# Eighteen steps of a 128-step product loop computed earlier, in plain fp32, kept in DRAM and read back

## The chip, the core and the metric

The kernel runs on one core of a Trainium2 chip. The metric is device time in microseconds (us). A profiled execution gives the trace that is read here. The engines are named as in the trace: PE (TensorE; PEld is its weight load), DVE (VectorE), ACT (ScalarE), POOL (GpSimd) and SP (the queue that issues most of the transfers). All data are 4-byte floats. Two kinds of product occur on PE: a plain fp32 product, and a product of operands that were cast to the format fp32r.

## The reference, cut to what matters

Two transformer blocks run one after the other on 512 tokens of 1024 channels. The change concerns the last layer, a sparse FFN with 16384 experts of one hidden unit each:

```python
q = (xb @ w_query).reshape(128, 8, 2, 128)
sc = einsum('thpd,hpkd->thpk', q, sub_keys)        # 128 keys in each half
s_top, i_top = lax.top_k(sc, 16)
...                                                # 16 best pairs per head, softmax g
u = jnp.take(expert_u, eidx, axis=0)               # 128 experts per token
h = jax.nn.gelu(jnp.einsum('thkd,td->thk', u, xb))
vv = jnp.take(expert_v, eidx, axis=0)
return jnp.einsum('thk,thkd->td', g * h, vv)
```

## The kernel before, in words

Everything ahead of `phase_d` is unchanged. `phase_d` computes the sparse FFN in three stages that overlap.

- **Query stage** (`d_norm`, `d_query`). The normed input is held transposed as a sum of two fp32r tiles, `hTh` (high part) and `hTl` (low part). PE makes the queries, and DVE finds the 16 best keys and pairs (`top16`, the tile `eq`).
- **Gate stage** (`d_gates`, three calls, one for each of the first three blocks of 128 tokens). For those 384 tokens the layer is computed densely: the gates are spread over all 128 x 128 experts. For each token a one-hot matrix `o1` and a weighted one-hot matrix `o2`, each 128 x 128, are made on ACT, POOL and DVE, and PE multiplies them into PSUM (`pw`, L1280; 384 products, of plain fp32). ACT copies the result to `wst` and SP writes it to DRAM (`w_d`, 12 transfers of 2 MB). Both `o1` and `o2` have three buffers, each for four tokens.
- **Main loop** over 128 steps s, each with 128 experts. SP loads 128 rows of `peer_v` (`vraw`) and, every fourth step, gates (`wb`). The activations `G` of the step are multiplied by the gates (`A`, DVE), both `vraw` and `A` are split into a high and a low fp32r part (`vh`, `vl`, `ah`, `al`), and PE adds 18 products of 512 columns into six PSUM banks (`pY`, L1146).

The activations of a step come from `h_step`: SP loads 128 columns of `peer_u` transposed (`uraw`, three buffers), ACT casts the high part `uh`, POOL subtracts to make the low part `ul` (L1061), PE makes 24 products of 384 columns (`ph`, L1088: hi x hi, hi x lo and lo x hi for eight blocks of channels), and ACT applies Gelu into `G` (L1091). `h_step` runs LA = 33 steps ahead of the step that uses it: the first 33 are written in the gate stage, the others one for each step of the main loop, as long as s + LA is below 128. `G` has LA + 1 buffers.

The last 128 tokens are done by gathering instead: POOL gathers 128 + 128 times one expert row for each token (`X`, `xg`; six buffers), and DVE makes one dot product (L1123) or one weighted sum (L1128) from each, called a dot below. These 256 dots are spread over the main loop by `done`: a step with an `h_step` has weight 2 in `cost`, a step without one has weight 1, and `q` advances by 260 times the share of the weights done so far. DVE's order within the main loop is as written (`manual_schedule`): `vl`, `A`, `al`, then the dots of the step. The other orders are set by a scheduler when the program is built, which may move instructions of later steps ahead where buffers allow.

Of the kernel before, what the change touches and what calls it, by code (L numbers as in the profile page):

```python
# [5 lines left out]
F32 = mybir.dt.float32  # L6
# [3 lines left out]
AF = mybir.ActivationFunctionType  # L10
# [147 lines left out]
class K:  # L158
# [904 lines left out]

    def phase_d(self):
        tc, nc, I, V, C, X = self.tc, self.nc, self.I, self.V, self.C, self.X
        ND, LA, NB, GL = 384, 33, 4, 5
        x_d = self.x_d
        self.w_d = self.dr.tile([32, 128, ND, 4], F32, name="w_d")
        with tc.tile_pool(name="d1", bufs=1) as d1, tc.tile_pool(name="hps", bufs=2, space=PSUM) as hps:
            hh = d1.tile([128, 8, 512], F32R, name="hTh")  # L1070
            hl = d1.tile([128, 8, 512], F32R, name="hTl")
# [8 lines left out]
            def h_step(s):  # L1080
                u = d1.tile([128, 8, 128], F32, name="uraw", bufs=3)
                nc.sync.dma_start(u.rearrange("p k e -> p (k e)"), I["put"][s])
                uh, ul = self.split(d1, "u", u, [128, 8, 128], eng=nc.gpsimd)
                p = hps.tile([128, ND], F32, name="ph")
                n = 0
                for k in range(8):
                    for l, r in ((uh, hh), (uh, hl), (ul, hh)):
                        nc.tensor.matmul(p, l[:, k, :], r[:, k, 0:ND], start=(n == 0), stop=(n == 23))  # L1088
                        n += 1
                G = d1.tile([128, ND], F32, name="G", bufs=LA + 1)  # L1090
                nc.scalar.activation(G, p, AF.Gelu_apprx_tanh)  # L1091
                return G

            with tc.tile_pool(name="dk", bufs=1) as dk, tc.tile_pool(name="kps", bufs=3, space=PSUM) as ps:
                self.ei = dk.tile([128, 4, 128], F32, name="ei")
                self.gt = dk.tile([128, 4, 128], F32, name="gt")
                self.arp = ps
                with tc.tile_pool(name="dn", bufs=1) as dn:
                    self.d_norm(dn, hh, hl, x3, h3)
                with tc.tile_pool(name="dq", bufs=1, reuse_waits="tile") as dq:  # L1100
                    self.d_query(dq, ps, hh, hl)
                with tc.tile_pool(name="dt", bufs=1, reuse_waits="tile") as dt:
                    for t in range(3):
                        self.d_gates(dt, ps, t)
                    Gs = {s: h_step(s) for s in range(LA)}

            def gather(tab, q):
                i = q % 6
                u = X[:, i, :] if i < 4 else xg[:, i - 4, :]
                nc.gpsimd.indirect_dma_start(out=u, out_offset=None, in_=tab,  # L1110
                                             in_offset=bass.IndirectOffsetOnAxis(ap=self.eix[q // 128][:, q % 128:q % 128 + 1], axis=0))
                return u

            with tc.tile_pool(name="dg", bufs=1) as dg, tc.tile_pool(name="yps", bufs=1, space=PSUM) as yps:
                xg = dg.tile([128, 2, 1024], F32, name="xg")
                ug = {}
                cost = [2 if s + LA < 128 else 1 for s in range(128)]
                done = lambda s: min(256, 260 * sum(cost[:s]) // sum(cost))

                def dot(q):  # L1120
                    u = ug.pop(q)
                    if q < 128:
                        nc.vector.scalar_tensor_tensor(u, u, 1.0, h3, op0=OP.mult, op1=OP.mult, accum_out=hv[:, q:q + 1])  # L1123
                        if q == 127:
                            nc.scalar.activation(hv, hv, AF.Gelu_apprx_tanh)
                            nc.vector.tensor_mul(hv, hv, self.g3)
                    else:
                        nc.vector.scalar_tensor_tensor(x3, u, hv[:, q - 128:q - 127], x3, op0=OP.mult, op1=OP.add)  # L1128

                pY = [[yps.tile([128, 512], F32, name=f"pY{t}{h}") for h in range(2)] for t in range(3)]  # L1130
                with tc.manual_schedule(engines={mybir.EngineType.DVE}):
                    for s in range(128):
                        vr = dg.tile([128, 1024], F32, name="vraw", bufs=3)
                        nc.sync.dma_start(vr, I["pv"][s * 128:s * 128 + 128, :])
                        if s % NB == 0:
                            wb = dg.tile([128, ND, NB], F32, name="wb", bufs=2)
                            nc.sync.dma_start(wb, self.w_d[s // NB])
                        vh, vl = self.split(dg, "v", vr, [128, 1024], bufs=3)
                        A = dg.tile([128, ND], F32, name="A", bufs=2)
                        nc.vector.tensor_mul(A, Gs.pop(s), wb[:, :, s % NB])  # L1140
                        ah, al = self.split(dg, "a", A, [128, ND], bufs=3)
                        for t in range(3):
                            for h in range(2):
                                n = 0
                                for l, r in ((ah, vh), (ah, vl), (al, vh)):
                                    nc.tensor.matmul(pY[t][h], l[:, t * 128:t * 128 + 128], r[:, h * 512:h * 512 + 512],  # L1146
                                                     start=(s == 0 and n == 0), stop=(s == 127 and n == 2))
                                    n += 1
                        if s + LA < 128:
                            Gs[s + LA] = h_step(s + LA)  # L1150
                        for q in range(done(s), done(s + 1)):
                            ug[q] = gather(I["pu"] if q < 128 else I["pv"], q)
                            if q >= GL:
                                dot(q - GL)
                for q in range(256 - GL, 256):
                    dot(q)
                nc.sync.dma_start(self.out[384:512, :], x3)
                for t in range(3):
                    xr = dg.tile([128, 1024], F32, name="vraw", bufs=3)
                    nc.sync.dma_start(xr, x_d[t * 128:t * 128 + 128, :])  # L1160
                    for h in range(2):
                        nc.vector.tensor_add(xr[:, h * 512:h * 512 + 512], xr[:, h * 512:h * 512 + 512], pY[t][h])
                    nc.sync.dma_start(self.out[t * 128:t * 128 + 128, :], xr)
# [147 lines left out]
```

## Time and profile before

| what | value |
|---|---|
| median of three runs | 3338.21 us (3332.45 to 3347.19) |
| the profiled execution: its own time | 3341.98 us |
| its span in the trace | 3340.2 us |
| mean granted TensorE clock | 0.971 of full speed |
| PE busy | 3072.6 us, 92% |
| DVE busy | 1834.3 us, 55% |
| POOL busy | 1144.9 us, 34% |
| ACT busy | 970.9 us, 29% |

Shares are of the whole span. Before about 1960 us the program does the other layers, which the change leaves alone. The query stage runs from about 2000 us, the products of the gate stage from 2272.7 to 2400.7 us, and the main loop from 2417.6 us to the end. In the trace each plain fp32 product shows as two MATMUL instructions, so the 384 products of the gate stage are counted there as 768; an fp32r product shows as one.

### The profile page before, as it was taken

The page shows a single profiled execution, that of the slowest core. Times are in us where ns is not written, and L with a number is a line of the kernel's source. Part 1 is how long each engine was busy: PE and PEld are TensorE (multiplying, and loading weights), DVE is VectorE, ACT ScalarE, POOL GpSimd, SP SyncE. Part 2 cuts the span into 40 slices and gives each one's busy share as a digit, 9 for nine tenths or more (in the row PEclk, how much of TensorE's full clock was granted, in tenths as well). Part 3 has the DMA queues.
Part 4 walks back from the last instruction along what each step waited for, and adds up shares of the span by engine and source line. Part 5 has one row for each costly group of instructions (what it writes and reads, how often), then busy time and mean ns, then how long its engine had stood idle before and what let it go on. Part 6 is the DMA issues. An engine that isn't in the chain of part 4 may idle for free.

```text
span 3340.2 us, 42188 instructions
## 1 busy us (share of the span) xinstructions
PE 3072.6 (92%) x16081; PEld 2166.9 (65%) x16081; DVE 1834.3 (55%) x3590; ACT 970.9 (29%) x1745; POOL 1144.9 (34%) x963
## 2 busy tenths in 40 slices
PE   7999999997888988988979989988799999999998
PEld 6777776572323323323337678887699999999986
DVE  2456656461000000000032658999799988989978
ACT  3333323130000000000022742237733333333332
POOL 0433321010000000000002122679778877777733
PEclk9999999988999999999989999999899999999999
DMA  4221112388999999999952152226788888888877
GB/s 144 104 74 58 61 68 72 109 310 349 427 427 427 427 426 427 428 426 427 427 198 76 44 180 87 76 101 190 226 303 311 310 305 299 303 295 303 285 264 260
DMA packets 193351, 837.85 MB, mean 251 GB/s; under 512 B 16509, under 2 KB 66301, under 8 KB 168446
## 3 DMA queue, kind: packets, MB, share of 16 engines
q1 hardware_dynamic: 153230, 693.52, 53.7%
q0 software_dynamic: 38592, 140.53, 11.9%
q8 instruction: 127, 2.08, 0.2%
q10 hardware_dynamic: 1328, 1.11, 0.1%
q14 instruction: 74, 0.61, 0.0%
HBM read 794.47 MB, written 40.63 MB: 250 GB/s over the span
## 4 chain that ended last, share of the span: by engine, by line
PE 71%; DMA 13%; DVE 11%; ACT 3%; issue 1%; POOL 1%; SPq 0%; DVEq 0%; ACTq 0%; POOLq 0%
PE pY L1146 14%; PE ph L1088 13%; PE pj L306 11%; DMA wt<-in_wu_dram 8%; PE pu L872 5%; PE pd L885 5%; PE pg L872 5%; DMA wt<-in_wg_dram 3%; PE pout L769 2%; PE po L897 2%; PE pj L468 1%; PE pq L626 1%; PE pw L1280 1%; DVE eq L1226 1%; DVE o L1278 1%
## 5 line engine op out<-in xcount | busy, mean ns | idle before, releaser
L876 DVE TENSOR_TENSOR sg<-sg,pu 128x512 f32<-128x512 f32 x32 | 22.0, 688 | 683.9 <-PE pu L872 683.9
L1061 POOL TENSOR_TENSOR ul<-uraw,uh 128x1024 fp32r<-128x1024 f32 x128 | 340.8, 2663 | 130.5 <-ACT uh L1058 128.9
L1088 PE MATMUL ph<-hTh,ul 128*128 128x384 f32 x1024 | 348.5, 340 | 18.3 <-POOL ul L1061 18.2
L1088 PE MATMUL ph<-hTh,uh 128*128 128x384 f32 x1024 | 347.4, 339 | 1.9 <-ACT G L1091 1.9
L1088 PE MATMUL ph<-hTl,uh 128*128 128x384 f32 x1024 | 346.1, 338 | 0.0
L1146 PE MATMUL pY<-vh,ah 128*128 128x512 f32 x768 | 302.4, 394 | 21.4 <-DMA vraw<-in_pv_dram 16.9
L1146 PE MATMUL pY<-vl,ah 128*128 128x512 f32 x768 | 300.7, 392 | 0.0
L872 PE MATMUL pu<-wt,xeT 128*64 128x512 f32 x1024 | 265.0, 622 | 37.4 <-DMA wt<-in_wu_dram 37.3
L1146 PE MATMUL pY<-vh,al 128*128 128x512 f32 x768 | 278.2, 389 | 0.0
L872 PE MATMUL pg<-wt,xeT 128*64 128x512 f32 x1024 | 254.5, 604 | 16.7 <-DMA wt<-in_wg_dram 16.7
L885 PE MATMUL pd<-wt,aT 128*64 128x512 f32 x1024 | 243.9, 597 | 22.6 <-ACT aT L881 22.6
L853 POOL DMA_INDIRECT xe<-h_d,idi x8 | 7.7, 957 | 613.8 <-PE pt L859 580.5
L306 PE MATMUL pj<-hh,wh 128*128 128x512 f32 x528 | 215.3, 408 | 1.8 <-DVE hl L205 1.1
L306 PE MATMUL pj<-hh,wl 128*128 128x512 f32 x528 | 216.3, 410 | 0.0
L872 PEld LDWEIGHTS pu<-wt,xeT 128*64 128x64 f32 x1024 | 86.9, 143 | 199.4 <-issue 148.7
L306 PE MATMUL pj<-hl,wh 128*128 128x512 f32 x528 | 214.5, 406 | 0.0
L1088 PEld LDWEIGHTS ph<-hTh,ul 128*128 128x128 f32 x1024 | 194.1, 190 | 22.9 <-POOL ul L1061 22.7
L1058 ACT CAST vh<-vraw 128x1024 fp32r<-128x1024 f32 x128 | 134.5, 1051 | 252.2 <-PE pY L1146 222.8
L872 PEld LDWEIGHTS pg<-wt,xeT 128*64 128x64 f32 x1024 | 88.0, 139 | 172.4 <-issue 139.5
L1088 PEld LDWEIGHTS ph<-hTh,uh 128*128 128x128 f32 x1024 | 194.3, 190 | 6.3 <-ACT G L1091 2.5
L1088 PEld LDWEIGHTS ph<-hTl,uh 128*128 128x128 f32 x1024 | 194.0, 189 | 3.8
L885 PEld LDWEIGHTS pd<-wt,aT 128*64 128x64 f32 x1024 | 88.8, 136 | 151.0 <-issue 121.0
(435 smaller groups left out, 6172.5 us busy)
## 6 DMA issues: line engine op xcount, KB each, us to landing
wt<-in_wg_dram SPq DMA_DIRECT2D x64, 2048.0 KB
wt<-in_wu_dram SPq DMA_DIRECT2D x64, 2048.0 KB
wt<-in_wd_dram SPq DMA_DIRECT2D x64, 2048.0 KB
uraw<-in_put_dram SPq DMA_DIRECT2D x128, 512.0 KB
vraw<-in_pv_dram SPq DMA_DIRECT2D x128, 512.0 KB
wraw<-in_w_in_dram SPq DMA_DIRECT2D x32, 1024.0 KB
w_d<-wst SPq DMA_DIRECT2D x12, 2048.0 KB
wb<-w_d SPq DMA_DIRECT2D x32, 768.0 KB
```

The costliest lines, as they stand in the source:

```text
L306: nc.tensor.matmul(p, l[:, k, :], r[:, k, :], start=(i == 0), stop=(i == 23))
L468: nc.tensor.matmul(pb, wb[:, k, f * 128:f * 128 + 128], y[:, k, :], start=(k == 0), stop=(k == nk - 1))
L626: nc.tensor.matmul(p[o:o + 64, h, :], lhs(h, o), rhs(h, o), start=True, stop=True)
L769: nc.tensor.matmul(pp[t][h], l[:, ts], r[:, hs], start=(k == 0 and i == 0), stop=(k == 7 and i == 2))
L872: nc.tensor.matmul(dst[e * 64:e * 64 + 64], xT[:, k, e * 64:e * 64 + 64], ww[e][:, k, :], start=(k == 0), stop=(k == 7))
L885: nc.tensor.matmul(pd[h][e * 64:e * 64 + 64], aT[:, k, e * 64:e * 64 + 64], wd[e][:, k, h * 512:h * 512 + 512], start=(c == 0 and k == 0), ...
L897: nc.tensor.matmul(po, oh[:, t * 128:t * 128 + 128], yes[h], start=True, stop=True)
L1058: nc.scalar.copy(hi, src)
L1061: (eng or nc.vector).tensor_sub(lo, src, hi)
L1088: nc.tensor.matmul(p, l[:, k, :], r[:, k, 0:ND], start=(n == 0), stop=(n == 23))
L1146: nc.tensor.matmul(pY[t][h], l[:, t * 128:t * 128 + 128], r[:, h * 512:h * 512 + 512], start=(s == 0 and n == 0), stop=(s == 127 and n == 2))
L1226: nc.vector.tensor_mul(eq, eq, ci[:, t:t + 1, :].to_broadcast([128, 16, NCAND]))
```

## The change

Eighteen steps, s = 35, 39, ..., 103 (`parked`), get their activations in another way. Behind the first LA `h_step`s, within the gate stage, `hTh` and `hTl` are added into one fp32 tile `hTf` (four adds on DVE, four on POOL). For each parked step `uraw` is loaded, PE makes eight plain fp32 products of 384 columns straight from `uraw` and `hTf`, ACT applies Gelu into `Gp` (two buffers), and SP writes it to DRAM (`g_d`). In the main loop, where a parked step's `h_step` stood, SP loads `G` from `g_d`. LA falls from 33 to 32, the parked steps get weight 1 in `cost`, and `G` has 33 buffers.

```diff
-        ND, LA, NB, GL = 384, 33, 4, 5
+        ND, LA, NB, GL = 384, 32, 4, 5
+        parked = range(LA + 3, LA + 3 + 4 * 18, 4)
+        g_d = self.dr.tile([128, 128, ND], F32, name="g_d")
...
                     Gs = {s: h_step(s) for s in range(LA)}
+                    hf = dt.tile([128, 8, ND], F32, name="hTf")
+                    for k in range(8):
+                        (nc.gpsimd if k % 2 else nc.vector).tensor_add(hf[:, k, :], hh[:, k, 0:ND], hl[:, k, 0:ND])
+                    for s in parked:
+                        u = d1.tile([128, 8, 128], F32, name="uraw", bufs=3)
+                        nc.sync.dma_start(u.rearrange("p k e -> p (k e)"), I["put"][s])
+                        p = hps.tile([128, ND], F32, name="ph")
+                        for k in range(8):
+                            nc.tensor.matmul(p, u[:, k, :], hf[:, k, :], start=(k == 0), stop=(k == 7))
+                        G = dt.tile([128, ND], F32, name="Gp", bufs=2)
+                        nc.scalar.activation(G, p, AF.Gelu_apprx_tanh)
+                        nc.sync.dma_start(g_d[s], G)
...
-                cost = [2 if s + LA < 128 else 1 for s in range(128)]
+                cost = [2 if s + LA < 128 and s + LA not in parked else 1 for s in range(128)]
...
-                        if s + LA < 128:
+                        if s + LA in parked:
+                            Gs[s + LA] = d1.tile([128, ND], F32, name="G", bufs=LA + 1)
+                            nc.sync.dma_start(Gs[s + LA], g_d[s + LA])
+                        elif s + LA < 128:
                             Gs[s + LA] = h_step(s + LA)
```

The lines below the change have higher numbers in the new kernel: L1088 becomes L1090, L1280 becomes L1297, L1146 becomes L1160.

The first place is PE's order where the gate products begin. Before, the last `h_step` products stand there and then gate products alone:

```order
4315 L1088 MATMUL ph<-hTh,uh 128x384
4316 L1088 MATMUL ph<-hTl,uh 128x384
4317 L1088 MATMUL ph<-hTh,ul 128x384
4318 L1280 MATMUL pw<-o_13143,o_13142 128x128 x4
4319 L1280 MATMUL pw<-o_13160,o_13159 128x128 x4
4320 L1280 MATMUL pw<-o_13177,o_13176 128x128 x4
4321 L1280 MATMUL pw<-o_13194,o_13193 128x128 x4
```

With the change the plain products (L1116, from `hTf` and `uraw`) alternate with them, ten between each twelve gate products further on:

```order
4210 L1090 MATMUL ph<-hTh,ul 128x384
4211 L1116 MATMUL ph<-hTf,uraw 128x384 x2
4212 L1273 MATMUL ptr<-con,f_i 128x128 x2
4213 L1273 MATMUL ptr<-con,gt 128x128
4214 L1116 MATMUL ph<-hTf,uraw 128x384 x12
4215 L1297 MATMUL pw<-o_13093,o_13092 128x128 x4
4216 L1297 MATMUL pw<-o_13110,o_13109 128x128 x4
4217 L1297 MATMUL pw<-o_13127,o_13126 128x128 x4
4218 L1116 MATMUL ph<-hTf,uraw 128x384 x2
4219 L1297 MATMUL pw<-o_13144,o_13143 128x128 x4
4220 L1297 MATMUL pw<-o_13161,o_13160 128x128 x4
4221 L1116 MATMUL ph<-hTf,uraw 128x384 x8
```

All 144 plain products stand among the first 200 of the 384 gate products, as do 72 products of the last three early `h_step`s; the other 184 gate products stand alone behind them. Ahead of the gate products stand 50 `h_step` products fewer than before (456 before, 406 now, in the last long row of them).

The second place is POOL's order in the main loop, where it alternates between gathers (`X`, `xg`) and `ul`. Before there is one `ul` for each step, with two or three gathers between:

```order
429 L1061 TENSOR_TENSOR ul<-uraw,uh 128x1024
430 L1110 DMA X<-in_pu_dram,eix_11227 128x1024 x2
431 L1061 TENSOR_TENSOR ul<-uraw,uh 128x1024
432 L1110 DMA X<-in_pu_dram,eix_11227 128x1024 x2
433 L1061 TENSOR_TENSOR ul<-uraw,uh 128x1024
434 L1110 DMA xg<-in_pu_dram,eix_11227 128x1024 x2
435 L1110 DMA X<-in_pu_dram,eix_11227 128x1024
436 L1061 TENSOR_TENSOR ul<-uraw,uh 128x1024
```

With the change one `ul` in four is gone in the first 72 steps, and up to five gathers stand in a row in its place:

```order
434 L1061 TENSOR_TENSOR ul<-uraw,uh 128x1024
435 L1124 DMA X<-in_pu_dram,eix_11228 128x1024 x4
436 L1124 DMA xg<-in_pu_dram,eix_11228 128x1024
437 L1061 TENSOR_TENSOR ul<-uraw,uh 128x1024
438 L1124 DMA xg<-in_pu_dram,eix_11228 128x1024
439 L1061 TENSOR_TENSOR ul<-uraw,uh 128x1024
440 L1124 DMA X<-in_pu_dram,eix_11228 128x1024 x2
441 L1061 TENSOR_TENSOR ul<-uraw,uh 128x1024
```

The third place is SP's queue in the main loop, here with the change: in a parked step a small load of `G` stands where a load of `uraw` stood.

```order
258 L1151 DMA wb<-w_d 128x1536
259 L1084 DMA uraw<-in_put_dram 128x1024
260 L1148 DMA vraw<-in_pv_dram 128x1024
261 L1084 DMA uraw<-in_put_dram 128x1024
262 L1148 DMA vraw<-in_pv_dram 128x1024
263 L1165 DMA G<-g_d 128x384
264 L1084 DMA uraw<-in_put_dram 128x1024
```

Before, loads of `uraw` and `vraw` alternate there without a break.

## Rows read from the trace of the kernel before

**Rows 1.** Busy time of each engine by stretch: gate stage, gap, main loop, tail.

```profile
core 0: us, PE busy (x) PEld busy (x) DVE busy (x) ACT busy (x) POOL busy (x), PEclk, DMA share, GB/s
2264.00:2401.00 137.00, 115.03 (x824) 104.31 (x822) 132.89 (x463) 119.84 (x319) 129.85 (x197) 0.96 0.68 198
2401.00:2418.00 17.00, 0.41 (x1) 0.41 (x2) 2.40 (x3) 2.31 (x4) 1.97 (x2) 0.58 0.84 273
2418.00:3190.00 772.00, 772.00 (x3917) 704.72 (x3917) 689.57 (x639) 276.87 (x377) 578.58 (x308) 1.00 0.85 301
3190.00:3335.00 145.00, 139.11 (x597) 111.78 (x595) 122.24 (x134) 46.91 (x61) 53.59 (x32) 0.99 0.74 265
```

**Rows 2.** Chain that ended last, main loop: start, us, engine, line, count.

```profile
2443.99 4.17 PE ph L1088 x24
2448.16 4.08 PE pY L1146 x18
```

**Rows 3.** PE's products of L1088 by stretch, before and in the main loop.

```profile
1960.00:2418.00 458.00, 163.17 (x864) 153.93 (x864) 0.96 0.44 141
2418.00:3335.00 917.00, 398.49 (x2208) 385.84 (x2208) 1.00 0.83 295
```

**Rows 4.** Timeline of PE: start, us, line, operation, count, idle time before.

```profile
2178.30 0.44 PE L1088 MATMUL ph<-hTh,uh 128*128 128x384 f32 x1 [1.18 <-ACT G L1091]
...
2263.91 0.38 PE L1256 MATMUL ptr<-con,f_i 128*128 128x128 f32 x2
...
2304.42 4.01 PE L1280 MATMUL pw<-o,o 128*128 128x128 f32 x32 [0.79 <-ACT o L1275]
...
2396.41 4.33 PE L1280 MATMUL pw<-o,o 128*128 128x128 f32 x32 [0.49 <-ACT o L1275]
...
2417.59 0.79 PE L1146 MATMUL pY<-vh,ah 128*128 128x512 f32 x1 [16.85 <-DMA vraw<-in_pv_dram]
```

**Rows 5.** PE's products of L1280 alone, in two stretches of the gate stage.

```profile
2320.00:2360.00 40.00, 34.90 (x256) 31.12 (x256) 1.00 0.73 205
2360.00:2400.00 40.00, 34.46 (x252) 31.14 (x252) 0.96 0.75 210
```

**Rows 6.** Plain fp32 products of another layer (24): durations, first and last start.

```profile
L468 PE MATMUL pj<-zrw,wb x48: 592/592/697, 626.0 to 646.2; 128*128 128x512 f32 x48
```

**Rows 7.** Timeline of POOL at the start of the gate stage.

```profile
2263.85 0.94 POOL L1110 DMA_INDIRECT X<-in_pu_dram,eix  x1 [0.30 <-issue]
2264.82 4.68 POOL L1061 TENSOR_TENSOR ul<-uraw,uh 128x1024 fp32r<-128x1024 f32 x2
```

**Rows 8.** Timeline of DVE in the main loop.

```profile
2603.81 1.21 DVE L1061 TENSOR_TENSOR vl<-vraw,vh 128x1024 fp32r<-128x1024 f32 x1
2604.95 0.84 DVE L1140 TENSOR_TENSOR A<-G,wb 128x384 f32<-128x384 f32 x1
2606.37 0.56 DVE L1061 TENSOR_TENSOR al<-A,ah 128x384 fp32r<-128x384 f32 x1 [0.58 <-ACT ah L1058]
2606.84 1.22 DVE L1123 SCALAR_TENSOR_TENSOR X<-X,h 128x1024 f32<-128x1024 f32 x1
2607.99 0.08 DVE L1123 DVE_READ_ACCUMULATOR X<-X,h 128x1 f32 x1
2607.99 3.43 DVE L1123 SCALAR_TENSOR_TENSOR X<-X,h 128x1024 f32<-128x1024 f32 x1
2611.34 0.08 DVE L1123 DVE_READ_ACCUMULATOR X<-X,h 128x1 f32 x1
2611.34 1.22 DVE L1061 TENSOR_TENSOR vl<-vraw,vh 128x1024 fp32r<-128x1024 f32 x1
```

**Rows 9.** Timeline of POOL in the same stretch of the main loop.

```profile
2607.37 2.96 POOL L1061 TENSOR_TENSOR ul<-uraw,uh 128x1024 fp32r<-128x1024 f32 x1 [0.75 <-ACT uh L1058]
2610.48 1.76 POOL L1110 DMA_INDIRECT X<-in_pu_dram,eix  x1
```

**Rows 10.** Timeline of DVE in the tail, where no `h_step` is left.

```profile
3211.54 1.28 DVE L1128 SCALAR_TENSOR_TENSOR x<-X,hv,x 128x1024 f32<-128x1024 f32 x1
3212.73 1.22 DVE L1061 TENSOR_TENSOR vl<-vraw,vh 128x1024 fp32r<-128x1024 f32 x1
...
3215.82 1.28 DVE L1128 SCALAR_TENSOR_TENSOR x<-X,hv,x 128x1024 f32<-128x1024 f32 x1
3217.01 1.22 DVE L1061 TENSOR_TENSOR vl<-vraw,vh 128x1024 fp32r<-128x1024 f32 x1
```

**Rows 11.** Transfers that SP issued at the end of the gate stage.

```profile
2401.39 0.36 SPq L1283 DMA_DIRECT2D w_d<-wst  x1
2410.25 0.34 SPq L1134 DMA_DIRECT2D vraw<-in_pv_dram  x1
```

## The prediction

> **What bounds the kernel now.** I read the busy time by stretch first [rows 1]. From 2418 to 3190 us PE is busy for all of 772 us: the main loop is bound by PE. DVE is busy there for 689.6 of 772 us, which is 89%. The gate stage, 2264 to 2401 us, is bound by no single engine: DVE is busy for 132.9 and POOL for 129.9 of 137 us, ACT for 119.8, PE for 115.0. Between the two lies a gap of 17 us in which PE does nothing. After 3190 us no `h_step` is left.
>
> The chain of waits gives the prices of the loop: 24 products of an `h_step` take 4.17 us, the 18 products of `pY` 4.08 us [rows 2], so a step is 8.25 us. Of the 128 `h_step`s 36 (864 products) are done before 2418 us and 92 (2208) in the loop [rows 3], since the scheduler moves three more ahead than are written in the gate stage. 92 x 4.17 + 128 x 4.08 = 906 us of PE work fill the 917 us from 2417.6 us to the end.
>
> DVE has to be looked at more closely, because its 89% leave out its waits. One step with two dots [rows 8]: from `vl` at 2603.81 to the next `vl` at 2611.34 is 7.53 us. One dot takes 1.15 us (2606.84 to 2607.99), the other 3.35 us (2607.99 to 2611.34), and while it lasts POOL does its `ul` (2607.37, 2.96 us) [rows 9]. Without dots the step is 7.53 - 1.15 - 3.35 = 3.03 us, DVE's wait of 0.58 us for `ah` included. So a step without dots costs DVE 3.03 us, a dot 1.15 us, and each `ul` of POOL lengthens one dot by 2.20 us. With 260/223 = 1.166 dots for each unit of weight, a step of weight 2 has 2.33 dots: 3.03 + 2.33 x 1.15 + 2.20 = 7.91 us, against PE's 8.25. DVE is only 4% behind PE.
>
> **The price of a plain product.** The kernel before has no plain product of 384 columns. The nearest row is one of 512 columns in another layer [rows 6]: 24 products show as 48 instructions, which start from 626.0 to 646.2 us, so one instruction follows the other after 20.2 / 47 = 0.430 us. Scaled to 384 columns that is 0.322 us, two of them 0.645 us for a product, and 8 x 0.645 = 5.16 us for a parked step. The split step that it replaces takes 4.17 us. The plain step saves the cast and the subtraction on ACT and POOL, but costs PE a quarter more. Over all: 144 x 0.645 = 92.9 us of PE work come, 18 x 4.17 = 75.1 us go.
>
> The Trainium skill states in FP8 and Floating Point Precision, TensorE Precision Notes, that true fp32 takes four passes through the array, and in TensorE: Matmul & The Clock Gate, Back-to-back issue gap, that a pass of N columns takes N/2.4 + 2.5 ns at the full clock. By these an fp32r product of 384 columns would take 162.5 ns, where the row has 4.17 / 24 = 174 ns; a plain one 650 ns; the 17 steps that leave the loop would be worth 66.3 us where the row makes 70.9, and the sum below would come out 5 us later. The measured row is used.
>
> **Gate stage: what is added.** First `hTf`: four adds on DVE and four on POOL. DVE's nearest row is `al` of the same size, 0.56 us [rows 8]. POOL does 1024 columns in 4.68 / 2 = 2.34 us [rows 7], so 384 in 0.9 us, and its adds stand behind four gathers of which the last ends at 2264.8 us. The first plain products can thus run from about 2266 us, where the transposes of the gates began at 2263.9 us [rows 4]. The 50 `h_step` products that no longer stand ahead of them (8.7 us) give nothing: PE waits for `hTf` and for DVE's query work.
>
> From 2266 us PE has, among the first 200 gate products: 92.9 us of plain products, 72 x 0.174 = 12.5 us of split products, and 200 gate products. A gate product is two instructions, and 32 of these take 4.01 to 4.33 us back to back [rows 4], so 0.26 us each, 52 us. Together 157.4 us. Before, gate products went at (256 + 252) / 2 = 254 in 80 us [rows 5], 0.315 us each, a pace that DVE, POOL and ACT set; for 200 that is 63 us. So here PE sets the pace and the others wait. With the three buffers of `o1` and `o2` they are ready for each group of twelve while PE does ten plain products (6.5 us). What PE may wait for is the Gelu that frees `ph` (two buffers): one such wait is 1.18 us [rows 4], so 0 to 21 us for 18 steps; I take 4 us, nearer to nothing, because a buffer is free for most of a step ahead. The 18 loads of `uraw` and 18 writes of `g_d` (13 MB) lie beside 157 us of PE work. The end of this part: 2266 + 157 + 4 = 2427 us. The other 184 gate products go as before, 184 x 0.315 = 58 us: 2485 us, where the last one now ends at 2400.7. **Plus 85 us** (81 to 102).
>
> The gap behind it stays: SP's last write of `w_d` is issued at 2401.39 us, the next load of `vraw` only at 2410.25 [rows 11], and the first `pY` starts at 2417.6 [rows 4]. The same writes and loads end the stage with the change.
>
> **Main loop: what is removed.** Early `h_step`s are 35 now (LA is one less), so 110 - 35 = 75 split steps stay in the loop, 17 fewer: 17 x 4.17 = 70.9 us of PE work. For PE alone that is the gain. But the dots remain 256 in number, and weights of 206 instead of 223 make it 1.262 for each unit. In four steps with one parked (weight 7, 8.83 dots) DVE needs 4 x 3.03 + 8.83 x 1.15 + 3 x 2.20 = 28.9 us, and PE 3 x 8.25 + 4.08 = 28.8. DVE's slack is gone. There are 18 such groups. They take DVE 520 us, PE only 506 us, as three steps were done early: 14 us are given back, and I add 5 us (an estimate, 0.3 us a group) for two engines that are both full and have three buffers between them. The 24 steps behind them have 2.52 dots, 8.13 us of DVE against 8.25 of PE. In the tail, one step with a dot is 4.28 us (3212.73 to 3217.01), its dot 1.19 us [rows 10]: 33 steps with 35 dots were 143.6 us, 32 with 37 are 142.9. So **minus 70.9 + 19 = minus 52 us** (minus 71 if DVE hides, minus 17 if the missing `ul` frees no dot: 18 x 2.2 = 40 us less, less the 14).
>
> The reload of `G` (192 KB instead of 512 KB of `uraw`) comes 32 steps ahead of its use. Four steps move 9.3 MB in 28.9 us, 321 GB/s, where the loop moves 301 at a DMA share of 0.85 [rows 1]; at the same price that is a share of 0.91, which I count at nothing.
>
> **The sum.** 3342.0 (the profiled execution's own time, 1.8 us over its span) + 85 - 52 = 3375 us. The median of the runs shown is 3.8 us lower, so I forecast 3372 us, 1.0% slower. Within 0.5%, 3321.5 to 3355 us, is about what a measurement of this kernel can't tell from no change.
>
> **Rivals.**
>
> *PE alone binds.* No waits in the gate stage and DVE hides in the loop: 81 - 71 = +10 us, 3348. Against it: rows 8 leave DVE no room. Chance 0.17.
>
> *Faster: a plain product takes one pass.* If it took as long as an fp32r one, 0.174 us, the first part of the gate stage would be 25 + 12.5 + 52 = 90 us, its end 2266 + 90 + 58 = 2414, +13 us; with -52 the time is 3299. It decides for faster below 0.30 us a product, where the gate stage grows by less than 35 us. Against it: the 48 instructions of 24 products, 0.430 us apart [rows 6]. Chance 0.04. By the four passes of the Trainium skill's FP8 and Floating Point Precision it would not come.
>
> *A convoy in the gate stage.* SP works in order: `uraw`, `g_d` and `w_d` wait there for one another, `Gp` has two buffers, and ACT's Gelu stands in line ahead of the casts for the next gate products. If each of 18 steps costs PE 1.2 us more and the writes of `w_d` hold `uraw` up now and then, the stage grows by 110 us: 3396. Chance 0.12.
>
> *The loop gives nothing back.* Up to five gathers in a row stand ahead of POOL's next `ul`, each waits for a dot, and PE waits for `ul`: with -17 the time is 3406. Chance 0.07.
>
> **How the numbers follow.** The forecast has 0.60, mostly from 3358 to 3388 us. The range of 3346 to 3402 reaches from the first rival into the last two and leaves out the fast one. Slower: 0.57 of the forecast and the last two, 0.76. Within 0.5%: the first rival and the rest of the forecast, 0.20. Faster: 0.04.
>
> **What would show it.** In the changed profile: instructions of L1116 about 0.32 us apart; the last gate product near 2485 us, with PE full and DVE, POOL and ACT waiting for PE up to about 2427; the gap of 17 us again; in the first 72 steps PE no longer full, waiting for `ah` behind DVE, four steps in about 29 us; and dots of 1.2 us only in parked steps. The forecast is wrong if the plain products cost PE much less than 5.2 us a step, if the gap closes, or if DVE keeps slack in the loop.

## The result and the profile after

| what | before | after |
|---|---|---|
| median, runs | 3336.16 us, 5 (3332.45 to 3347.19) | 3368.27 us, 5 (3365.99 to 3377.96) |
| profiled execution, span | 3341.98 us, 3340.2 us | 3377.96 us, 3376.2 us |

The ratio is 1.0093, interval 1.0079 to 1.0107: the changed kernel is 32 us slower, forecast 3372 us.

The two profiled executions can't be laid on each other directly: the layers ahead of the change took 8 us longer in that of after. The first query product (`pj<-hTh,wqh`) serves as a common mark. Each line has an instruction's count, its shortest, median and longest duration in ns, and its first and last start. They show, for the kernel before and then for after, this mark and the products of the main loop, and for after also the plain and the gate products:

```profile
L1192 PE MATMUL pj<-hTh,wqh x128: 389/395/480, 1999.1 to 2101.1; 128*128 128x512 f32 x128
...
L1146 PE MATMUL pY<-vh,al x768: 387/389/397, 2423.2 to 3333.2; 128*128 128x512 f32 x192
```

```profile
L1209 PE MATMUL pj<-hTh,wqh x128: 389/395/480, 2007.0 to 2108.3; 128*128 128x512 f32 x128
...
L1116 PE MATMUL ph<-hTf,uraw x288: 486/486/847, 2266.4 to 2401.2; 128*128 128x384 f32 x144
...
L1297 PE MATMUL pw<-o,o x768: 270/275/524, 2280.7 to 2482.4; 128*128 128x128 f32 x192
...
L1160 PE MATMUL pY<-vh,ah x768: 387/389/793, 2499.6 to 3367.9; 128*128 128x512 f32 x192
...
L1160 PE MATMUL pY<-vh,al x768: 387/389/628, 2505.6 to 3369.5; 128*128 128x512 f32 x192
```

From the mark to the first `pY` it is 2417.6 - 1999.1 = 418.5 us before [rows 4] and 2499.6 - 2007.0 = 492.6 us after: **gate stage +74 us**. The main loop, from the first `pY` to the last, goes from 3333.2 - 2417.6 = 915.6 to 3369.5 - 2499.6 = 869.9 us: **-46 us**. The rest of the 36 us between the two executions is the 8 us ahead of the mark; the medians are 32 us apart.

Busy time by stretch in after, which answers to [rows 1]: plain products, the rest of the gate stage, the gap, and the loop in three parts, cut where PE starts steps 72 and 96 (the first 72 steps are those with parked ones, and from step 96 on, in the tail, no `h_step` is left). Below it are the same three parts of the loop in before.

```profile
core 0: us, PE busy (x) PEld busy (x) DVE busy (x) ACT busy (x) POOL busy (x), PEclk, DMA share, GB/s
2266.00:2402.00 136.00, 132.90 (x625) 93.29 (x626) 67.83 (x226) 63.62 (x162) 65.34 (x97) 0.99 0.57 176
2402.00:2483.00 81.00, 70.92 (x513) 65.89 (x512) 71.32 (x248) 68.45 (x178) 72.43 (x109) 0.98 0.74 211
2483.00:2500.00 17.00, 0.45 (x1) 0.45 (x2) 2.44 (x3) 2.28 (x4) 1.97 (x2) 0.61 0.83 278
2499.60:3018.50 518.90, 511.36 (x2521) 456.83 (x2522) 469.83 (x502) 174.56 (x248) 381.53 (x204) 1.00 0.89 316
3018.50:3221.20 202.70, 199.32 (x1010) 180.78 (x1009) 186.11 (x137) 67.50 (x97) 164.00 (x86) 1.00 0.86 304
3221.20:3369.70 148.50, 136.95 (x577) 109.06 (x575) 122.36 (x132) 45.69 (x60) 58.50 (x35) 0.98 0.75 266
```

```profile
2417.60:3000.50 582.90, 582.90 (x2952) 531.81 (x2953) 526.43 (x519) 209.74 (x287) 445.35 (x235) 1.00 0.86 305
3000.50:3194.30 193.80, 193.80 (x987) 176.91 (x986) 166.55 (x123) 67.94 (x92) 135.22 (x75) 1.00 0.81 284
3194.30:3333.40 139.10, 134.59 (x577) 108.19 (x575) 117.63 (x128) 46.42 (x60) 51.60 (x31) 0.99 0.76 271
```

While plain products run, PE is busy for 133 of 136 us and the other three for half of it, where before they were busy for 87 to 97% of the stage. In the loop PE is no longer full: it is idle for 7.5, 3.4 and 11.6 us in the three parts, where before it was idle in the tail alone, for 4.5 us.

PE's timeline in the gate stage of after (start, us, line, operation, count, idle time before):

```profile
2266.39 1.53 PE L1116 MATMUL ph<-hTf,uraw 128*128 128x384 f32 x4 [3.04 <-issue]
2268.44 0.41 PE L1273 MATMUL ptr<-con,f_i 128*128 128x128 f32 x2 [0.52 <-DVE e_i L1267]
...
2271.14 9.70 PE L1116 MATMUL ph<-hTf,uraw 128*128 128x384 f32 x24 [2.19 <-POOL hTf L1110]
...
2294.28 6.62 PE L1116 MATMUL ph<-hTf,uraw 128*128 128x384 f32 x20
2300.73 2.84 PE L1297 MATMUL pw<-o,o 128*128 128x128 f32 x24
2303.41 6.62 PE L1116 MATMUL ph<-hTf,uraw 128*128 128x384 f32 x20
```

Ten plain products take 2300.73 - 2294.28 = 6.45 us, 0.645 each; the twelve gate products behind them 2.68 us, 0.223 each, with no wait between.

Who waits in this stage, 2266 to 2483 us of after (us, times, longest):

```profile
POOL o L1290 <- PE pw L1297: 63.6, 15, 6.1
DVE o L1290 <- PE pw L1297: 55.7, 13, 5.4
ACT wst L1298 <- PE pw L1297: 43.1, 23, 9.3
ACT Gp L1118 <- PE ph L1116: 29.9, 12, 4.0
```

These, the four longest waits of the stage, are all for PE. A wait of PE for a Gelu does not occur in this stage.

DVE's timeline in the loop of after, which answers to [rows 8]: a parked step, then a step with an `ul` beside it; then POOL's in the same stretch, as [rows 9], and one row of PE's.

```profile
2703.21 1.22 DVE L1061 TENSOR_TENSOR vl<-vraw,vh 128x1024 fp32r<-128x1024 f32 x1
...
2706.28 1.22 DVE L1137 SCALAR_TENSOR_TENSOR X<-X,h 128x1024 f32<-128x1024 f32 x1
...
2707.42 1.22 DVE L1137 SCALAR_TENSOR_TENSOR X<-X,h 128x1024 f32<-128x1024 f32 x1
...
2708.57 1.22 DVE L1137 SCALAR_TENSOR_TENSOR X<-X,h 128x1024 f32<-128x1024 f32 x1
...
2709.72 1.22 DVE L1061 TENSOR_TENSOR vl<-vraw,vh 128x1024 fp32r<-128x1024 f32 x1
...
2728.21 1.22 DVE L1137 SCALAR_TENSOR_TENSOR X<-X,h 128x1024 f32<-128x1024 f32 x1
...
2729.36 3.43 DVE L1137 SCALAR_TENSOR_TENSOR X<-X,h 128x1024 f32<-128x1024 f32 x1
...
2732.71 1.22 DVE L1061 TENSOR_TENSOR vl<-vraw,vh 128x1024 fp32r<-128x1024 f32 x1
```

```profile
2707.78 1.68 POOL L1124 DMA_INDIRECT X<-in_pu_dram,eix  x1 [1.77 <-DVE X L1137]
...
2713.00 2.39 POOL L1061 TENSOR_TENSOR ul<-uraw,uh 128x1024 fp32r<-128x1024 f32 x1
...
2728.74 2.96 POOL L1061 TENSOR_TENSOR ul<-uraw,uh 128x1024 fp32r<-128x1024 f32 x1 [0.33 <-ACT uh L1058]
```

```profile
2715.44 0.45 PE L1090 MATMUL ph<-hTh,ul 128*128 128x384 f32 x1 [0.89 <-POOL ul L1061]
```

In the parked step three dots take 1.15 us each, with gathers of POOL beside the second and the third; in the other step the dot beside `ul` takes 3.35. Four steps, 2703.21 to 2732.71, take 29.5 us, and DVE has no idle time in them but the 0.6 us a step in which it waits for `ah`.

PE's own waits show how this reaches it. In the first 96 steps of after it waits 14 times, 10.9 us in all, each time for an `ul` of POOL and never for `ah`. In the rows above, POOL's gather at 2707.78 had waited 1.77 us for a dot on DVE to free its buffer; with five gathers ahead of it the `ul` came at 2713.00, and PE stood for 0.89 us.

### The profile page after: what moved, and what is told of

Read it like the earlier page. It is cut to its first block, busy times and chain, and to the rows that moved or that the text cites. A ratio compares the mean times of both kernels' runs of the same rounds, so it can differ in the third digit from the quotient of the medians.

```text
span 3376.2 us, 41928 instructions
## 1 busy us (share of the span) xinstructions
PE 3094.0 (92%) x15937; PEld 2146.1 (64%) x15937; DVE 1804.7 (53%) x3594; ACT 943.0 (28%) x1727; POOL 1114.1 (33%) x949
## 3 DMA queue, kind: packets, MB, share of 16 engines
q10 hardware_dynamic: 1328, 1.11, 0.1%
## 4 chain that ended last, share of the span: by engine, by line
PE 55%; DVE 16%; DMA 13%; issue 9%; POOL 4%; ACT 3%; SPq 0%; DVEq 0%; ACTq 0%; POOLq 0%
PE pj L306 11%; DMA wt<-in_wu_dram 8%; PE pd L885 5%; PE pu L872 5%; PE pg L872 4%; PE pY L1160 4%; DMA wt<-in_wg_dram 3%; PE ph L1116 3%; DVE X L1137 2%; PE ph L1090 2%; PE pout L769 2%; DVE vl L1061 2%; PE po L897 2%; PE pw L1297 2%; POOL X L1124 2%
## 5 line engine op out<-in xcount | busy, mean ns | idle before, releaser
L1160 PE MATMUL pY<-vh,ah 128*128 128x512 f32 x768 | 303.6, 395 | 28.4 <-ACT ah L1058 28.4
L1090 PE MATMUL ph<-hTh,ul 128*128 128x384 f32 x880 | 301.3, 342 | 27.7 <-POOL ul L1061 27.5
L1061 POOL TENSOR_TENSOR ul<-uraw,uh 128x1024 fp32r<-128x1024 f32 x110 | 298.3, 2712 | 63.8 <-ACT uh L1058 63.2
L1160 PE MATMUL pY<-vl,ah 128*128 128x512 f32 x768 | 301.9, 393 | 0.0
L1090 PE MATMUL ph<-hTh,uh 128*128 128x384 f32 x880 | 298.9, 340 | 1.2 <-ACT G L1093 1.2
L1090 PE MATMUL ph<-hTl,uh 128*128 128x384 f32 x880 | 297.6, 338 | 0.0
L1160 PE MATMUL pY<-vh,al 128*128 128x512 f32 x768 | 277.2, 389 | 0.0
L1058 ACT CAST ah<-A 128x384 fp32r<-128x384 f32 x128 | 65.7, 513 | 522.8 <-DVE A L1154 516.0
L1090 PEld LDWEIGHTS ph<-hTh,ul 128*128 128x128 f32 x880 | 166.6, 189 | 37.0 <-POOL ul L1061 36.6
L1160 PEld LDWEIGHTS pY<-vh,ah 128*128 128x128 f32 x768 | 145.8, 190 | 60.6 <-ACT ah L1058 33.5
L1061 DVE TENSOR_TENSOR vl<-vraw,vh 128x1024 fp32r<-128x1024 f32 x128 | 161.8, 1264 | 17.1 <-ACT vh L1058 17.1
```

The lines of the kernel that those rows point to most:

```text
L1061: (eng or nc.vector).tensor_sub(lo, src, hi)
```

## The experiments

Theory: the gate stage takes the plain products almost in full because PE binds it there, and the loop returns less than PE is spared because DVE's 256 dots, stretched by POOL's `ul`, then set its pace. Rivals: the loop is held by something else (gathers, transfers, the reload of `G`); the price is that of fp32 and not of moving work; the two parts are not independent.

For each kernel the table has the median, the ratio to before with its interval, and from its trace the time from the mark to the first `pY`, the length of the loop, and PE's own work in the loop: split `h_step`s left in it (counted by the products of `h_step`) times 4.17 us, and 128 x 4.08 = 522 us for `pY`.

| kernel | median us | ratio | mark to `pY` | loop | PE's work in the loop |
|---|---|---|---|---|---|
| before | 3336 to 3340 | | 418.5 | 915.6 | 92 steps, 906 |
| after | 3368.27 | 1.0093 [1.0079, 1.0107] | 492.6 | 869.9 | 75, 835 |
| e1 | 3419.58 | 1.0238 [1.0221, 1.0255] | 493.2 | 919.8 | 93, 910 |
| e2 | 3291.54 | 0.9851 [0.9834, 0.9867] | 417.0 | 869.4 | 75, 835 |
| e3 | 3344.17 | 1.0010 [0.9999, 1.0021] | 468.1 | 866.7 | 75, 835 |
| e7 | 3351.27 | 1.0037 [1.0023, 1.0052] | 434.3 | 905.7 | 89, 893 |
| e4 | 3332.54 | 0.9983 [0.9972, 0.9995] | 492.6 | 836.5 | 75, 835 |
| e5 | 3328.54 | 0.9962 [0.9946, 0.9977] | 417.7 | 907.3 | 92, 906 |
| e6 | 3335.62 | 0.9985 [0.9975, 0.9994] | 417.5 | 907.4 | 92, 906 |
| e8 | 3322.82 | 0.9952 [0.9936, 0.9968] | 442.5 | 877.5 | 84, 873 |
| e9 | 3349.41 | 1.0034 [1.0022, 1.0047] | 507.3 | 836.1 | 75, 835 |
| e10 | 3344.90 | 1.0021 [1.0009, 1.0033] | 494.9 | 844.3 | 75, 835 |

**e1: the gate part alone.** The plain steps stay, but their results go to rows of the output that are overwritten later, and the loop makes all its activations itself.

```diff
-                        nc.sync.dma_start(g_d[s], G)
+                        i = (s - LA - 3) // 4 % 8
+                        nc.sync.dma_start(self.out[i // 2 * 128:i // 2 * 128 + 128, i % 2 * ND:i % 2 * ND + ND], G)
...
-                        if s + LA in parked:
...
-                        elif s + LA < 128:
+                        if s + LA < 128:
```

> The gate stage's part of the change alone: the 18 plain steps are computed there and written to DRAM (into the output's rows, which the end of the kernel writes again), but the main loop makes all its activations itself, as before (LA 32). My theory, that the plain products cost PE its time in the gate stage: first product of the main loop at about 2500 us, as with the whole change, 82 us later than before; the loop then as before, one split step longer (921 us); in all about 3420 us. A rival by which the two parts hang together (the gate stage is longer only because the loop's reloads and loads come into its queues) has the gate stage end near 2418 us and about 3340 us.

Measured +75 us in the gate stage and +4 in the loop, which is the one `h_step` more that LA = 32 leaves there.

**e2: the loop part alone.** No plain step; the loop loads `G` from rows of `peer_u` in the same size, so the activations of the parked steps are other numbers.

```diff
-                            nc.sync.dma_start(Gs[s + LA], g_d[s + LA])
+                            nc.sync.dma_start(Gs[s + LA], I["put"][s + LA, :, 0:ND])
```

> The main loop's part alone: no plain steps, nothing parked; in the loop the 18 steps read their activations from part of the input instead (so the values are others), with the change's weights and LA 32. My theory: the gate stage as before (first product of the loop at about 2416 us), the loop 870 us as with the whole change and not 847, because DVE takes over in the first 72 steps (29.5 us for four steps against PE's 28.8); about 3288 us. The rival by which PE alone binds the loop: 917 - 71 = 846 us for the loop, about 3264 us. The rival by which the loop gives nothing back: over 3310 us.

Measured -46 us in the loop, -1.5 in the gate stage. The loop of e2 is that of after to within 0.5 us, so it does not matter that the loads come from a `g_d` written before, and the two parts add up. e2 has loads of the same size; that these cost the loop nearly nothing follows from e4 below, which has them and comes within 1.5 us of PE's work.

**e3: the parked steps in split form.** The cast, the subtraction and 24 fp32r products in place of `hTf` and eight plain products.

```diff
+                        uh, ul = self.split(d1, "u", u, [128, 8, 128], eng=nc.gpsimd)
-                            nc.tensor.matmul(p, u[:, k, :], hf[:, k, :], start=(k == 0), stop=(k == 7))
+                            for l, r in ((uh, hh), (uh, hl), (ul, hh)):
+                                nc.tensor.matmul(p, l[:, k, :], r[:, k, 0:ND], start=(n == 0), stop=(n == 23))
```

> As the whole change, but the 18 parked steps are computed in the gate stage by the three split products (24 of 174 ns) instead of eight plain ones, and parked in DRAM in the same way. My theory, that the price is PE time: 18 x (5.16 - 4.17) = 18 us less in the gate stage, about 3351 us, still slower than before. If the price is the parking (writes, loads, waits of ACT and SP): no less than 3368 us, or more, since ACT and POOL get 18 casts and 18 subtractions more (19 and 43 us).

The gate stage is 24.5 us shorter than in after. By the price, 17.8 us of this are 18 x (5.16 - 4.17). Another 5.2 are that PE doesn't wait for `hTf` at the start: its first parked product starts 2255.4 - 1999.0 = 256.4 us behind the mark, in after 259.4 us, with another 2.2 us of waiting for `hTf` behind it. Where the last 1.5 us come from was not traced. So three quarters of the loss (24 of 32 us by the medians) are the plain form. Moving the steps is then worth nothing: +50 in the gate stage, -49 in the loop.

**e4 and e5: dots over half the columns,** in after and in before; the sums over the other 512 columns are left out.

The weighted sums are cut in the same way.

```diff
-                        nc.vector.scalar_tensor_tensor(u, u, 1.0, h3, op0=OP.mult, op1=OP.mult, accum_out=hv[:, q:q + 1])
+                        nc.vector.scalar_tensor_tensor(u[:, 0:512], u[:, 0:512], 1.0, h3[:, 0:512], op0=OP.mult, op1=OP.mult, accum_out=hv[:, q:q + 1])
```

> The changed kernel with each of the 256 dots over 512 of 1024 columns (the other half is left out), so DVE has about 0.55 us less for each dot and PE, POOL and the transfers the same. My theory, that DVE took over the loop: four steps with one parked go back to PE's 28.8 us from 29.5, the 12 us of the early split steps come back, the tail goes to PE's 4.1 us a step: the loop takes about 843 us instead of 870, in all about 3341 us. The rival by which PE alone binds the loop: the first 72 steps stay at 29.5 us for four, only the tail is shorter, about 3358 us.

> The kernel before with the same half dots (the other half is left out). My theory: there DVE has 4% slack, so the first 95 steps stay as they are (33.0 us for four), and only the tail is shorter: 33 steps at 4.1 instead of 4.3 to 4.6 us, 8 to 10 us less, about 3327 us. If DVE bound the loop before as well, the first 95 steps get shorter too: under 3318 us.

Busy time in the loop of e4, in the same three parts as above:

```profile
2486.40:2994.70 508.30, 508.30 (x2521) 457.18 (x2522) 297.27 (x508) 186.83 (x251) 304.21 (x208) 1.00 0.92 328
2994.70:3192.60 197.90, 197.90 (x1009) 181.03 (x1008) 107.20 (x133) 71.11 (x95) 122.10 (x83) 1.00 0.87 303
3192.60:3323.10 130.50, 130.50 (x577) 107.94 (x576) 102.02 (x132) 45.39 (x59) 49.38 (x33) 1.00 0.83 295
```

With the same gathers, the same transfers (328 GB/s instead of 316 in the first part) and the same `ul`, PE is full again and the loop is 836.5 us, 1.5 over PE's work. So the dots' time on DVE held the loop of after, for 33 us, where 27 were expected: 10.6 us in the first 72 steps (508.3 instead of 518.9), 4.8 in the next 24 (197.9 instead of 202.7) and 18.0 in the tail (130.5 instead of 148.5). In before the same cut (e5) changes nothing in the first 96 steps and gains 8 us in the tail: there DVE did not bind but at the end. The 33 us less these 8 are the 25 us that PE was spared in after and the loop did not return, 71 less 46.

The cut frees the gathers' buffers sooner as well, so it does not tell by which path the dots hold PE. The rows of after show PE waiting for an `ul` that stands behind gathers; an order of POOL with the `ul` ahead of them was not tried.

**e6: other weights, in before.** A step with an `h_step` has weight 3 instead of 2, so fewer dots are left for the tail.

```diff
-                cost = [2 if s + LA < 128 else 1 for s in range(128)]
+                cost = [3 if s + LA < 128 else 1 for s in range(128)]
```

> The kernel before with weight 3 instead of 2 for a step that has its split step, so that more of the dots stand where DVE has slack: 2.45 instead of 2.33 in such a step (8.05 us of DVE against PE's 8.25), 0.82 instead of 1.17 in a step of the tail (4.06 us against PE's 4.08). My theory: 8 to 10 us less in the tail, nothing lost ahead of it, about 3327 us. The rival: DVE's slack of 0.3 us a step is needed for the unevenness between steps of two and three dots, and the first 95 steps get longer: 3336 us or more.

The loop got 8 us shorter, all of it in the tail, as expected. The time did not follow: 3327 us was expected, and the median is 3335.62 against 3338.03 of the before run beside it, 2.4 us less (by the ratio 5 us), a gain below the 0.5% that counts here. The rival's sign, longer first steps, did not occur either.

**e7: four parked steps** instead of eighteen, plain.

```diff
-        parked = range(LA + 3, LA + 3 + 4 * 18, 4)
+        parked = range(LA + 3, LA + 3 + 4 * 4, 4)
```

> As the whole change, with 4 parked steps instead of 18. My theory: 4 x 5.16 = 20.6 us of PE come in the gate stage, which ends about 15 us later since a little of it falls into PE's idle time; three split steps less in the loop, 12.5 us, and DVE keeps slack there: +2 to +6 us, about 3340 us. If the cost goes with the number alone: 32 x 4 / 18 = +7 us. If few steps fit into PE's idle time (22 us in the gate stage): -10 us, about 3326 us.

Gate stage +15.8 us, loop -9.9: in the gate stage the loss scales with the number of steps, 3.9 us a step here and 4.1 in after. PE's 22 idle us there did not swallow even 20.6 us of plain products. The sum of the stages is +6, as expected; the medians differ by 11.5, more than expected, since the profiled execution was the fastest of its five (3348.3) and that of before lies 2 us over the median.

**e8: nine parked steps, split, weights 5 to 2.**

```diff
-        parked = range(LA + 3, LA + 3 + 4 * 18, 4)
+        parked = range(LA + 3, LA + 3 + 8 * 9, 8)
...
-                cost = [2 if s + LA < 128 and s + LA not in parked else 1 for s in range(128)]
+                cost = [5 if s + LA < 128 and s + LA not in parked else 2 for s in range(128)]
```

> Only nine steps are parked (35, 43, ..., 99), each by the 24 split products, and the weights of the dots are 5 (a step with an h_step) to 2. Theory (both parts scale: the gate stage has room for some PE work, since PE there is idle for 22 of 137 us in the kernel before, and DVE sets the loop's gain): nine parked steps bring 9 x 4.17 = 37.5 us of PE work into the gate stage, which gets 18 to 27 us longer (the 18 split steps: 49.6 us); the loop loses 8 x 4.17 = 33 us of PE work, of which DVE takes back some 5. Time 3322 to 3334 us, a little below the kernel before. Rival (the gate stage grows by all that is put into it, and the loop gives back only the part that DVE lets through): +37 - 28 = +9, 3345 us or more.

Faster than both kernels, by 14.7 us (0.5%) against before. Its gate stage grows by 24 us, in the range of the theory. Busy time in the loop of e8, in the same three parts:

```profile
2438.80:2985.60 546.80, 546.78 (x2737) 495.49 (x2738) 495.11 (x512) 185.95 (x266) 427.18 (x222) 0.99 0.89 314
2985.60:3184.70 199.10, 198.49 (x1010) 180.96 (x1009) 183.27 (x134) 68.33 (x99) 163.47 (x85) 1.00 0.85 305
3184.70:3316.50 131.80, 131.80 (x577) 107.39 (x575) 111.66 (x124) 45.65 (x60) 43.94 (x27) 1.00 0.74 266
```

PE is idle for 0.6 us in all, so the loop returned all of the eight steps, 33 us, and 5 more from the tail, where the theory had let DVE take 5 back. e8 changes the number of steps and the weights at once; what each of them gave was not told apart.

**e9 and e10: part of the dots made in the gate stage,** 40 in after (weights 3 to 1) and 16 in the split version e3 (weights 5 to 2). Each is a gather on POOL and a dot on DVE, written behind the parked steps and set among them and the gate products by the scheduler.

```diff
+                    for q in range(E0):
+                        ug[q] = X[:, q % 4, :]
+                        nc.gpsimd.indirect_dma_start(out=ug[q], out_offset=None, in_=I["pu"], in_offset=...)
+                        if q >= 3:
+                            dot(q - 3)
...
+                done = lambda s: min(256, E0 + (260 - E0) * sum(cost[:s]) // sum(cost))
```

> The changed kernel, with 40 of the 256 dots and their gathers done in the gate stage, where DVE and POOL have 75 us each of 161 left over while PE makes the plain products; the loop's weights are 3 to 1 for the 216 dots that remain. Theory (dots bind the loop, and the gate stage there is bound by PE): 40 dots cost DVE 46 to 90 us beside PE, so the gate stage stays within 10 us of the changed kernel's, and the loop falls from 870 to about 840 us, groups of four to 28.8 us: time 3335 to 3348 us. Rival (DVE's in-order stream delays the one-hot matrices behind dots that wait for their gathers): the gate stage gets longer by as much as the loop gains or more, 3365 us or above.

> The eighteen parked steps by 24 split products, 16 of the 256 dots done in the gate stage, and weights 5 to 2 for the other 240. Theory (dots bind the loop, the gate stage has room beside PE): the loop falls from 866.7 to 845 to 852 us, the gate stage grows by 0 to 8 us over that of the split version: time 3326 to 3336 us, below both kernels. Rival (POOL, busy for 105 of 120 us in that stretch of the split version, binds the gate stage): what the loop gains is lost there, 3342 us or above.

In both the loop gains what the theory says (836.1 us, 1.1 over PE's work; 844.3, 9.3 over). In e9 the gate stage pays 15 us for 34, more than the 10 expected, and the time ends 19 us below after, just above the range. One wait of 7.5 us, of PE's transposes for `e_i` on DVE, is half of the 15. In e10 the theory falls: the gate stage pays 27 us for 22, and nothing is left over e3. Busy time at the start of the gate stage, in e3 and then in e10:

```profile
2268.00:2330.00 62.00, 62.00 (x428) 62.00 (x428) 49.93 (x133) 46.92 (x108) 54.88 (x64) 0.98 0.66 210
```

```profile
2268.00:2330.00 62.00, 49.13 (x281) 46.26 (x282) 54.96 (x104) 25.24 (x56) 58.74 (x51) 0.92 0.68 227
```

With split steps POOL (54.9 of 62 us, `ul` in it) and DVE (49.9) have little room. With the dots put in they are at 58.7 and 55.0 and PE, full in e3, loses 13 us. Over the whole gate stage PE's waits in e10 grow for all three engines: for `o` of DVE from 0.6 to 7.7 us, for `o` of ACT from 8.5 to 11.8, for POOL's `ul` from 0.8 to 4.2. So no single engine is shown to bind e10. That e9 pays less because its plain form has no `ul` is argued and was not tried by itself.

## Why the prediction was right, point by point

- **Price of a plain product: right.** 0.645 us, as scaled from [rows 6]. By the four passes of the Trainium skill's FP8 and Floating Point Precision, TensorE Precision Notes, and the gap of TensorE: Matmul & The Clock Gate, Back-to-back issue gap, the estimate is 4 x 162.5 ns = 0.650. The trace agrees with that time; it shows two instructions for a product and not four, and an fp32r product, for which the gap gives 162.5 ns, takes 174 here. e3 shows what the form costs: 18 us of PE time and some 5 us of waiting for `hTf`.
- **PE binds the gate stage: right; the size was 11 us off.** "Plus 85 us" measured +74 (+75 in e1). The first plain product came 259.4 us behind the mark; the prediction's 2266 us on the clock of before is 266.9, so 7.5 us too late. The step that failed is that the 50 `h_step` products that no longer stand ahead "give nothing". Gate products indeed start no sooner without plain steps (2269.8 - 1996.3 = 273.5 us behind the mark in e2, 2272.7 - 1999.1 = 273.6 before). But plain products did not have to wait for them or for the transposes: PE was done with the split products ahead 8.6 us sooner behind the mark than before, and after 3 us of waiting for `hTf` the plain products stepped ahead of both. From the first plain to the last gate product it is 216 us, forecast 219. That this fits so well is partly luck, as two errors cancel inside. Only 164 gate products (328 instructions) and almost none of the 72 split products lie among the plain ones, which end at 2401 us and not 2427, and a gate product costs 0.223 us there, not 0.26. The 220 left need 81 us behind them and not 58, as 220 x 0.315 + 70 x 0.174 = 81.5. The wait of 4 us for a Gelu did not come; about 5 us for `hTf` did.
- **The gap of 17 us: right**, 2482.4 to 2499.6.
- **The loop: the next bound right, the path and the parts not; 6 us off in all.** "Minus 52 us" measured -46. Four steps take 29.5 us on DVE (28.9 and 0.3 for unevenness forecast), dots of 1.15 us stand free in parked steps (short dots stand in other steps too, at 2728.21 above and already in [rows 8], so "only in parked steps" was a poor sign), and e4 and e5 show that DVE's dots took the 25 us that PE was spared but the loop did not return. Of these, 19 were forecast, all in the first 72 steps, and they lie elsewhere. The first 72 steps have 18 split steps fewer, 75.1 us of PE work, and went from 582.9 to 518.9 us, so 11 us are missing there. The next 24 have one split step more, 4.2 us, and went from 193.8 to 202.7, so 5 are missing where nothing was forecast. The tail went from 139.1 to 148.5, where 0.7 us less was forecast. So the sum came near by errors of both signs. The path was another one, too: the prediction has PE waiting for `ah` behind DVE in the first 72 steps, and there all its waits are for `ul` behind gathers, the path of the fourth rival; `ah` holds PE only in the tail.
- **What failed in the tail** is the price of a second dot. A step with one dot takes the 4.28 us of [rows 10] (four take 17.1 in e8), but four steps with five dots take 20.0 to 20.5 us on DVE in the tail of after, where 4 x 4.28 + 1.19 = 18.3 follows from the prediction. Rows of DVE, ACT and PE in the tail of after, and the granted clock before, in and after this stretch:

```profile
3270.96 2.60 DVE L1142 SCALAR_TENSOR_TENSOR x<-X,hv,x 128x1024 f32<-128x1024 f32 x2
...
3276.64 1.04 ACT L1058 CAST vh<-vraw 128x1024 fp32r<-128x1024 f32 x1 [4.90 <-DMA vraw<-in_pv_dram]
...
3273.36 1.52 PE L1160 MATMUL pY<-vh,al 128*128 128x512 f32 x6
3278.15 0.50 PE L1160 MATMUL pY<-vh,ah 128*128 128x512 f32 x1 [3.27 <-ACT ah L1058]
...
3279.20 0.63 PE L1160 MATMUL pY<-vl,ah 128*128 128x512 f32 x1
3279.63 0.63 PE L1160 MATMUL pY<-vh,ah 128*128 128x512 f32 x1
```

```profile
3270.00:3274.00 4.00, 4.00 (x18) 3.11 (x17) 3.48 (x4) 1.50 (x2) 1.49 (x1) 1.00 0.85 308
3274.00:3278.10 4.10, 0.88 (x4) 0.38 (x2) 1.45 (x2) 1.46 (x2) 1.96 (x2) 1.00 0.85 297
3278.20:3282.00 3.80, 3.80 (x10) 2.98 (x11) 3.58 (x4) 0.14 (x1) 1.67 (x1) 0.56 0.39 148
```

  A step with two dots ends at 3273.5 on DVE, ACT's next `vh` then waits 4.9 us for its `vraw`, and PE stands for 3.27 us; behind the pause the clock is granted at 0.56, near its lower level of 1.2 GHz, and products start 0.43 us apart instead of 0.23. There are five such pauses in the tail of after (11.6 us together) and three in before (4.5 us). Each comes directly behind a step with two dots: behind steps 108, 112, 116, 120 and 124 in after, behind 109, 115 and 121 in before. Gates are loaded every fourth step in both, and in before the pauses are six steps apart, so that load does not set them. With weights 5 to 2 (e8), one dot a step, there is none, and the tail takes 131.8 us. That the second dot delays `vraw` by freeing its buffer late is argued from the order of the rows and was not tried by itself.
- **The rivals.** PE alone binds: refuted by e4 against after. One pass: refuted by 0.645 us. A convoy: it did not come; PE waits 5 us for `hTf` at the start and 10 us for `o` behind the plain products, and for no Gelu. A loop that gives nothing back: its path is there, but its size is not, as PE waits for `ul` for 7.5 us in the first 72 steps. All of it together gives +28 us between the marks of the two executions against +32 between the medians; the 4 us between are in the scatter of the layers ahead and of the runs.

## What to carry to other kernels

When the bound engine is given less work, look for the next engine before the gain is counted. Here DVE was 4% behind PE, and of the 71 us that PE was spared the loop returned 46. With less of DVE's work in the loop (e4, e9) it returned all of them, and so it did when fewer steps were moved and the dots weighted otherwise (e8, 33 of 33 us). The engine that sets the pace need not be the one that the bound engine is seen waiting for: DVE's dots held POOL's gathers, and PE waited for POOL.

Moved work costs in its new place by its form. Split steps added two thirds of their PE time to the gate stage (24 us for 37.5 in e8, 50 for 75 in e3), plain ones about four fifths (16 for 20.6 in e7, 74 for 93 in after). The 22 us in which PE was idle there did not take up even the four plain steps of e7 (20.6 us, of which 16 were paid). A plain fp32 product in place of three fp32r ones spares the other engines and costs PE a quarter more, which is a bad trade where PE is the bound.

## What the runs showed of the hardware

Not only the long dots are stretched beside POOL's `ul`. In the gate stage of e10, where DVE makes one-hot matrices (`o`, 128 x 128) while POOL works, DVE's timeline and POOL's:

```profile
2277.59 1.11 DVE L1305 TENSOR_SCALAR o<-con,trs 128x128 f32<-128x128 f32 x4
...
2285.98 3.80 DVE L1305 TENSOR_SCALAR o<-con,trs 128x128 f32<-128x128 f32 x4
```

```profile
2276.54 1.76 POOL L1135 DMA_INDIRECT X<-in_pu_dram,eix  x1 [0.15 <-PE ph L1128]
...
2287.36 2.34 POOL L1061 TENSOR_TENSOR ul<-uraw,uh 128x1024 fp32r<-128x1024 f32 x1
```

Four of them take 1.11 us next to a gather, and 3.80 us when an `ul` of 2.34 us falls among them: the loss, 2.69 us, is a little more than the whole of `ul`. The Trainium skill's SBUF — State Buffer, Who interferes with whom, has this as an exclusive hold of a port pair that the two engines share, for DVE instructions with two inputs in SBUF and for some others; the dots beside `ul` (3.43 us for 1.22) and beside a gather (1.22) agree with it.
